# Keys of the second group before the last norm, a split stage of its own, and output weights cast on another engine

## The chip, the cores and the metric

One NeuronCore of one Trainium2 chip runs the whole program. The metric is device time in microseconds of that core, as the median of several executions. Engine names are those of the profile: PE is TensorE's matmul, PEld its weight load, DVE VectorE, ACT ScalarE, POOL GpSimd, and SP the engine that issues most DMAs.

## What is computed

One step of a small encoder: 1024 prompt frames and 32 sample frames, stored together as 1056 columns, model width 1024, two layers. Layer 0 is an mLSTM mixer with a SwiGLU feed-forward; layer 1 is windowed attention with a shared key and value projection, 16 query heads over 2 key heads, a bias per distance and a sink per head, and again a SwiGLU feed-forward. Each sub-layer ends with a LayerNorm.

```python
q = (x @ w_q).reshape(B, nc, CHUNK, N_KV_HEADS, GROUP, HEAD_DIM)
s = einsum('bcqhgd,bckhd->bchgqk', q, k) * HEAD_DIM ** -0.5 + bias
mx = maximum(max(s), sink); p = exp(s - mx)
p = p / (sum(p) + exp(sink - mx))
o = einsum('bchgqk,bckhd->bcqhgd', p, v)
x = layer_norm(alpha * x + o.reshape(B, T, D_ATT) @ w_out, ln_g, ln_b)
```

All of it is float32. The kernel gets that precision from a faster matmul format: every operand is written as a rounded part (hi) and the rest (lo), and each product is three matmuls, hi by hi, hi by lo, lo by hi (lines 416 to 418).

## The kernel before

**Groups and tiles.** The 1056 columns are cut into three groups (0 to 383, 384 to 767, 768 to 1055) for projections, and into four quarters of 264 columns for the norms and the output projection. A projection of one weight tile over one group is 8 steps over the inner dimension, each of three matmuls: 24 matmuls.

**Weave.** All work is issued by one Python program, and the order in which it is issued is the order of each engine's queue. `gemm` (line 408) calls `wv.tick(us)` behind each step of three matmuls, with a nominal time for these. A tick lets side tasks (generators) run whose pauses have run out, and also the weight feed. `wv.drain` runs a task to its end at once. So the pauses of a task fix where, among the matmuls, its instructions stand.

**Weights.** `Weights._next` (line 219) loads a raw tile by SP, casts half of it to the rounded part (hi) and subtracts that to get lo. The cast is on ACT (line 245), or on POOL (line 243) for the halves named in `on_gpsimd`; the subtraction is on POOL, or on DVE for those named in `on_vector` (line 247). Five pairs of buffers hold the results.

**The end of layer 0.** `ffn` leaves four norm tasks, one for each quarter. While the last of them run, the layer-1 projections begin: `keys_values(0)` makes keys and values of group 0, four `q_group(j, 0)` make queries. `tasks[2]` and `tasks[3]`, the norms of quarters 2 and 3, are then drained, the PSUM pool of five banks is closed, and three pools are opened in its place: three banks for projections ("d"), two for scores ("psS", cleared in six single columns by DVE, line 1764), two for transposes ("T") and one for attention outputs ("O").

**The start of attention.** `k_spread` copies each key group to other partitions by six DMAs from SP. It is drained for group 0, then two tasks start: `v_turn(0, 3.0)`, which transposes the values of group 0 into T tiles, of which there are two, and has ACT and DVE split them (lines 1784, 1712 and 1713), and `attention`, which first pauses 4.0. Then `keys_values(1)` and `keys_values(2)` make the keys and values of groups 1 and 2, eight steps each.

**The attention pipeline** (line 1800) goes over 72 items, a head pair's half (j) and a block of 128 rows (b). Its stages: `scores` (PE matmuls into psS, DVE adds the bias and takes the minimum, line 1835), `soft` (ACT exponentials, line 1850), `scale` (DVE reciprocal, and a multiplication that is POOL's for blocks 1 to 7, line 1863), `turn` (PE transposes into a T tile, line 1888, and right behind them the ACT cast to hi, line 1892, and the DVE subtraction to lo, line 1893), `values` (PE matmuls of hi and lo, line 1917, for every second item) and `place` (ACT copy and DVE add). Between rounds it visits the stages in the order given by the last argument: place, turn, scale, soft, scores, values. A pause of 0.46 follows scores and turn.

**The output.** `mixed_parts` splits the attention result into hi and lo (lines 446 and 447, low part on DVE and POOL in turn), `out_tile` multiplies it by the output weights `U_OUT_B[0]` (first two quarters) and `U_OUT_B[1]` (last two). The first three (`EARLY`) tiles of quarter 0 are made between the query projections, the other five while the last attention items run.

Of the kernel before, what the change touches and what calls it, by code (L numbers as in the profile page):

```python
# [16 lines left out]
P = 128  # L17
# [3 lines left out]
DEC = 32  # L21
# [10 lines left out]
EARLY = 3  # L32
# [258 lines left out]
def kernel(ctx: ExitStack, tc: tile.TileContext, A, O):  # L291
    nc = tc.nc
    ctx.enter_context(tc.manual_schedule())
    wv = Weave()
# [11 lines left out]
    def new(p, tag, shape, dt=F32, bufs=1):  # L306
        uid[0] += 1
        return p.tile(list(shape), dt, name=f"{tag}_{uid[0]}", tag=tag, bufs=bufs)
# [45 lines left out]
    U_KV, U_QB, U_OUT_B = [], [[], []], [[], []]  # L354
# [11 lines left out]
    on_vector.update((u, f) for u in U_OUT_B[1][2:] for f in range(2))  # L366
    on_vector.update((u, f) for u in U_Q[:1] for f in range(2))
    on_gpsimd = {(u, 1) for u in U_KV[1] + U_QB[0][4:]}
    on_gpsimd.update((u, f) for u in U_QB[1] + U_OUT_B[0] for f in range(2))
    W = Weights(nc, base, units, pairs, on_vector, on_gpsimd)  # L370
    W.early = {up[i] for up in U_UP for i in range(FIRST, FT)}
    wv.feed = W.feed
# [875 lines left out]
    def out_tile(u, m, cols):  # L1248

        ps = psbank()[:, :N4]  # L1250
        gemm(ps, wcols(u), [(SX[:, 0, k, cols], SX[:, 1, k, cols]) for k in range(KT)])
        z = ACT[:, m, cols]
        nc.vector.scalar_tensor_tensor(z, z, ALPHA, ps, op0=ALU.mult, op1=ALU.add)

    def mixer_out(us, li, lx, opening=None, before=None, made=0):

        box = [lx]

        def run(g, cols, after):
            if before:  # L1260
                before(g)
            if g == 3:
                lx = box[0]
                lx.sums = ExitStack()
                su = lx.sums.enter_context(pool("sums"))
                bufs = [new(su, f"su{i}", [P, 2, N4])[:] for i in range(2)]
                wv.drain(lx.norms[1])
                lx.comb = wv.launch(sums(lx, li, 0, bufs, 2.4))

            order = [6, 7, *range(6)] if g == 3 and not opening else list(range(KT))  # L1270
            for i, m in enumerate(order):
                if not g and m < made:
                    continue
                u = us[g > 0][m]
                W.get(u)
                if g < 2:
                    W.split_to(us[g][min(m + 2, KT - 1)])
                out_tile(u, m, cols)
                if g == 3 or u not in us[1]:
                    W.done(u)  # L1280
                if g == 3 and (u, 0) in W.home:
                    box[0].left += 1
                if box[0]:
                    after(order, i)
            if not box[0]:
                box[0] = opening()
                for i in range(KT):
                    after(order, i)

        return norm_tail(li, run, box), box[0]  # L1290
# [326 lines left out]
    def parts_made(g):  # L1617
        wv.drain(parts, lambda: nparts[0] > g)

    tasks, lx = mixer_out(U_OUT_A, 0, lx, None, lambda g: g < 3 and parts_made(g))  # L1620
    tasks = ffn(0, 1, tasks, lx, False)
# [22 lines left out]
    def k_part(src, c0, n):  # L1644

        dst = slice(c0, c0 + n)
        nc.scalar.copy(KH[0][:, dst], src)
        nc.vector.tensor_sub(KL[0][:, dst], src, KH[0][:, dst].bitcast(F32))
# [60 lines left out]
    def v_parts(c, src, L):  # L1709

        src = src.rearrange("p (g d) -> p g d", g=2)
        nc.scalar.copy(VR[:L, c, :, 0, :], src)
        nc.vector.tensor_sub(VR[:L, c, :, 1, :], src, VR[:L, c, :, 0, :].bitcast(F32))
# [12 lines left out]
    def load_sample_bias(jp):  # L1726

        sb = SB[jp] = new(pb, "sb", [2 * DEC, 2, P + DEC + 1])
        nc.sync.dma_start(sb[:, :, 1:], A["sbias"][:, 2 * jp : 2 * jp + 2, :])
        for h in range(2):  # L1730
            r = slice(DEC * h, DEC * h + DEC)
            nc.gpsimd.tensor_copy(sb[r, :, 0], nsink[r, 4 * jp + h : 4 * jp + 4 : 2])
# [1 line left out]
    load_bias(0)  # L1734
    load_bias(1)
    load_sample_bias(0)
    def keys_values(g):
        if g == 2:
            k_part(ck[:], SEQ, P)
        for f, w in ((k_group, U_KV[g > 0][0]), (v_group, U_KV[g > 0][1])):  # L1740
            f(g)
            if g != 1:
                W.done(w)

    W.pause = 1.3
    for t in tasks[:2]:
# [3 lines left out]
        q_group(j, 0)  # L1750
        W.done(U_QB[0][j])
    W.pause = FEED_W
    for t in tasks[2:]:
        wv.drain(t)
    lx.close()
    lx.zx.close()
    psx[0].close()
# [13 lines left out]
    def pad_values(i, c, g2):  # L1771

        r = slice(64 * i, 64 * i + 64)
        nc.gpsimd.tensor_copy(VZ[i][r, c - 1 + i], VR[r, c, g2].rearrange("p a d -> p (a d)").bitcast(F32))

    def v_turn(group, pause):
        yield pause
        if not group:
            for i in range(2):
                nc.gpsimd.memset(VZ[i][64 * (1 - i) : 64 * (2 - i)].bitcast(F32), 0.0)  # L1780
        for c, c0, L, g, off in CH:
            if g == group:
                pt = new(psb, "T", [P, 512], bufs=2)
                nc.tensor.transpose(pt[:L, :P], vT[g][:, off : off + L], ident[:])
                v_parts(c, pt[:L, :P], L)
                for i in range(2):
                    if 1 - i <= c < 8 - i:
                        pad_values(i, c, 0)
                ast["v"] = c + 1
                yield 0.8  # L1790
# [6 lines left out]
    def last_item(j, g):  # L1797
        return 6 * JG.index((j // 2, g)) + 6

    def attention(gap):  # L1800
        S, pairs_ = {}, {}
# [67 lines left out]
        def blocks(b):  # L1869

            if b == 0:
                return [(1, 130, 64), (2, 258, P)]
            if b == 8:
                return [(0, 2, P), (1, 130, DEC)]
            return [(t, 2 + t * P, P) for t in range(3)]

        def turn(j, b):
            s = S.pop((j, b))
            p = s["p"]
            rows = 2 * DEC if b == 8 else P  # L1880
            if j % 2 == 0:
                pairs_[j // 2, b] = {
                    tag: new(pb2, tag, [P, 2, 3, P], F32R, bufs=2) for tag in ("hi", "lo")
                }
            s = pairs_[j // 2, b]
            pt = new(psb, "T", [P, 512], bufs=2).rearrange("p (t r) -> p t r", t=4)
            for t, at, nk in blocks(b):
                nc.tensor.transpose(pt[:nk, t, :rows], p[:rows, at : at + nk], ident[:rows, :rows])  # L1888
            cuts = [(slice(0, 3), P)] if 0 < b < 8 else [(slice(t, t + 1), nk) for t, _, nk in blocks(b)]
            hi, lo = (s[x][:, j % 2] for x in ("hi", "lo"))  # L1890
            for t, nk in cuts:
                nc.scalar.copy(hi[:nk, t, :rows], pt[:nk, t, :rows])
                nc.vector.tensor_sub(lo[:nk, t, :rows], pt[:nk, t, :rows], hi[:nk, t, :rows].bitcast(F32))
# [25 lines left out]
        def place(j, b):  # L1919
# [12 lines left out]
            for h in range(2):  # L1932
# [4 lines left out]
        always = lambda j, b: True  # L1937
# [5 lines left out]
                (soft, always, 0, 0),  # L1943
                (scale, always, 0, 0),
                (turn, always, 2, (gap,) * 8),
                (values, lambda j, b: ast["v"] > b, 1, (0.0, 2 * gap) * 4),
                (place, always, 0, 0),
            ],
            (5, 3, 2, 1, 0, 4),
        )  # L1950


    for t in spread:
        wv.drain(t)
    wv.launch(v_turn(0, 3.0))
    task = wv.launch(attention(GAP_A))
    ast["ready"] = 4
    for g in range(1, 3):
        keys_values(g)
        wv.launch(v_turn(g, 2.5))  # L1960
    for t in spread:
        wv.drain(t)
# [6 lines left out]
    def q_made():  # L1969
        yield 2.5  # L1970
        ast["ready"] += 1

    def before(g):
        if g == 0:
            wv.drain(task, lambda: ast["placed"] >= last_item(7, 0))
        if g < 3:
            parts_made(g)

    for n, (jp, g) in enumerate(JG):
        if n < 2:  # L1980
            continue
        while ast["scored"] < 6 * (n - 1):
            wv.tick(0.25)
        for j in (2 * jp, 2 * jp + 1):
            q_group(j, g)
            wv.launch(q_made())
            if g != 1:
                W.done(U_QB[g > 0][j])
        if n == 3:
            nparts[0] = 0  # L1990
            parts = wv.launch(
                mixed_parts(
                    scr,
                    lambda g: ast["ready"] > QG.index((7, g)),
                    lambda k, g: ast["placed"] >= last_item(k, g),
                    (2.4, 1.5, 1.5, 1.0, 1.0),
                    (nc.vector, nc.gpsimd),
                    [WHOLE[0], *((g, ks) for ks in (range(6), range(6, KT)) for g in (1, 2))],
                )
            )  # L2000
        if g == 2 and jp < EARLY:
            before(0)
            out_tile(U_OUT_B[0][jp], jp, QUARTERS[0][0])
            W.done(U_OUT_B[0][jp])
# [6 lines left out]
    tasks, lx = mixer_out(U_OUT_B, 2, None, finish, before, EARLY)  # L2011
# [133 lines left out]
```

## Time and profile before

| what | value |
|---|---|
| time, median of 3 runs | 2206.42 us (2204.69 to 2207.07) |
| profiled execution, its own time | 2207.18 us |
| its span in the trace | 2205.4 us |
| PE busy | 2168.4 us, 98% of the span |
| DVE, ACT, POOL busy | 1445.6, 990.7, 976.1 us |

A line of a timeline gives the start in microseconds, the duration, the engine, the line of the kernel and the operation, then output tile and input tiles, and in brackets the idle time before it with what ended it. A line of a table of groups gives the busy sum and the mean of one in ns. `d` is a projection's PSUM tile, `sx` the split activations, `wh` and `wl` (and `oh`, `ex`) split weights, `Q` queries, `KH` and `KL` split keys, `T` transposed tiles, `s` scores and probabilities.

### The profile page before, as it was taken

How to read it: one execution, taken by the hardware profiler on the slowest of the kernel's cores; microseconds unless marked ns; L12 is line 12 of the kernel's file. 1: busy time of each engine (PE TensorE's matmuls, PEld its weight loads, DVE VectorE, ACT ScalarE, POOL GpSimd, SP SyncE). 2: the span in 40 equal slices, each digit the busy share in tenths (PEclk: the TensorE clock that was granted, in tenths of full speed). 3: DMA queues.
4: the chain of work that ended last, by engine and by line, in shares of the span. 5: the costliest groups of instructions: out<-in, count | busy, mean ns of one | idle time of the engine just before them, and what ended most of it. 6: DMA issues, size and time to landing. Idle time of an engine off the chain costs nothing.

```text
span 2205.4 us, 43768 instructions
## 1 busy us (share of the span) xinstructions
PE 2168.4 (98%) x16982; PEld 2141.5 (97%) x16982; DVE 1445.6 (66%) x2818; ACT 990.7 (45%) x2229; POOL 976.1 (44%) x986
## 2 busy tenths in 40 slices
PE   9999999999999999999998999899999999999997
PEld 9999999999999999999998999899999999999997
DVE  4465576787656665566667777788666566467657
ACT  4443455465444444322236676656444444332125
POOL 2554310004655565544526665600666555554441
PEclk9999999999999999999999999999999999999999
DMA  5222212212443443697515321411344434397712
GB/s 170 77 63 57 58 40 87 89 39 77 158 146 138 146 156 137 229 334 232 180 64 151 94 71 51 137 59 39 120 154 156 146 133 151 137 346 252 246 57 80
DMA packets 166192, 289.97 MB, mean 131 GB/s; under 512 B 16416, under 2 KB 121944, under 8 KB 165984
## 3 DMA queue, kind: packets, MB, share of 16 engines
q1 hardware_dynamic: 161632, 282.84, 38.4%
q10 hardware_dynamic: 4352, 4.33, 0.6%
q8 instruction: 134, 2.20, 0.4%
q14 instruction: 74, 0.61, 0.1%
HBM read 202.35 MB, written 82.94 MB: 129 GB/s over the span
## 4 chain that ended last, share of the span: by engine, by line
PE 88%; DVE 6%; ACT 3%; issue 1%; DMA 1%; POOL 1%; SPq 0%; ACTq 0%; DVEq 0%; POOLq 0%
PE d L416 10%; PE d L418 10%; PE d L417 10%; PE A L416 10%; PE A L418 10%; PE A L417 10%; PE B L416 7%; PE B L417 7%; PE B L418 7%; PE O L1917 1%; PE psS L1829 1%; PE T L1888 1%; ACT act L519 1%; DMA hs_x<-z 1%; PE T L969 1%
## 5 line engine op out<-in xcount | busy, mean ns | idle before, releaser
L247 POOL TENSOR_TENSOR wl_s<-wr,wh_s 128x512 fp32r<-128x512 f32 x224 | 304.3, 1368 | 237.4 <-ACT wh_s L245 168.9
L416 PE MATMUL d<-sx,wh 128*128 128x264 f32 (+2 forms) x1040 | 333.5, 321 | 2.9 <-DVE Q L1699 2.2
L247 POOL TENSOR_TENSOR wl_a<-wr,wh_a 128x512 fp32r<-128x512 f32 x112 | 153.2, 1371 | 402.2 <-ACT wh_a L245 396.9
L418 PE MATMUL d<-sx,wl 128*128 128x264 f32 (+2 forms) x1040 | 317.4, 305 | 1.0 <-POOL wl L247 1.0
L417 PE MATMUL d<-sx,wh 128*128 128x264 f32 (+2 forms) x1040 | 316.9, 305 | 0.4 <-DVE sx L447 0.4
L416 PE MATMUL A<-sx,wh_s 128*128 128x264 f32 x896 | 254.5, 284 | 0.0
L417 PE MATMUL A<-sx,wh_s 128*128 128x264 f32 x896 | 254.1, 284 | 0.0
L418 PE MATMUL A<-sx,wl_s 128*128 128x264 f32 x896 | 254.0, 283 | 0.0
L245 ACT CAST wh_s<-wr 128x512 fp32r<-128x512 f32 x224 | 135.9, 619 | 192.4 <-DVE wr L197 102.8
L416 PEld LDWEIGHTS d<-sx,wh 128*128 128x128 f32 x1040 | 197.0, 189 | 6.6 <-ACT act L519 2.5
L417 PEld LDWEIGHTS d<-sx,wh 128*128 128x128 f32 x1040 | 197.3, 190 | 1.5 <-DVE sx L447 0.7
L418 PEld LDWEIGHTS d<-sx,wl 128*128 128x128 f32 x1040 | 196.4, 189 | 1.8 <-POOL wl L247 1.5
L416 PE MATMUL d<-sx,ex 128*128 128x264 f32 x624 | 180.7, 290 | 0.1
L418 PE MATMUL d<-sx,ex 128*128 128x264 f32 x624 | 177.0, 284 | 0.7 <-DVE ex L247 0.7
L417 PE MATMUL d<-sx,ex 128*128 128x264 f32 x624 | 177.2, 284 | 0.0
L418 PEld LDWEIGHTS A<-sx,wl_s 128*128 128x128 f32 x896 | 168.8, 188 | 0.0
L417 PEld LDWEIGHTS A<-sx,wh_s 128*128 128x128 f32 x896 | 168.4, 188 | 0.0
L416 PEld LDWEIGHTS A<-sx,wh_s 128*128 128x128 f32 x896 | 168.4, 188 | 0.0
L1346 POOL TENSOR_TENSOR z<-z 128x528 fp32r<-128x528 f32 x76 | 103.5, 1361 | 126.0 <-ACT z L1345 112.9
L247 POOL TENSOR_TENSOR wl<-wr,wh 128x512 fp32r<-128x512 f32 (+2 forms) x84 | 108.9, 1302 | 85.6 <-ACT wh L245 82.8
L416 PE MATMUL A<-ex,wh_s 128*128 128x264 f32 x448 | 127.5, 285 | 0.0
L417 PE MATMUL A<-ex,wh_s 128*128 128x264 f32 x448 | 127.1, 284 | 0.0
(377 smaller groups left out, 7213.4 us busy)
## 6 DMA issues: line engine op xcount, KB each, us to landing
wr<-in_gu SPq DMA_DIRECT2D x92, 512.0 KB, 4.7
hs_x<-z SPq DMA_DIRECT2D x72, 528.0 KB, 3.0
hs_t<-z SPq DMA_DIRECT2D x64, 528.0 KB, 2.8
sx<-hs_x SPq DMA_DIRECT2D x112, 264.0 KB, 5.9
sx<-hs_t SPq DMA_DIRECT2D x64, 264.0 KB, 6.2
ex<-hs_t SPq DMA_DIRECT2D x64, 264.0 KB, 6.6
wr<-in_dn SPq DMA_DIRECT2D x32, 512.0 KB, 3.9
ex<-hs_x SPq DMA_DIRECT2D x32, 264.0 KB, 5.4
```

What stands on the lines that cost most here:

```text
L245: self.nc.scalar.copy(hi, r)
L247: eng.tensor_sub(lo, r, hi.bitcast(F32))
L416: nc.tensor.matmul(out, ah, bh, start=start and k == 0, stop=False, **kw)
L417: nc.tensor.matmul(out, ah, bl, start=False, stop=False, **kw)
L418: nc.tensor.matmul(out, al, bh, start=False, stop=stop and k == last, **kw)
L519: nc.scalar.activation(z, z, AF.Identity, scale=gk, bias=bk)
L969: nc.tensor.matmul(pc[:, : 2 * (DV + 1)], keys, vt[j][:, c], start=True, stop=True)
L1346: eng.tensor_sub(lo.bitcast(F32R), buf(s), hi)
L1829: nc.tensor.matmul(ps[:rows, at : at + nk], lhs, k[:, k0 : k0 + nk], start=i == 0, stop=i == 1)
L1888: nc.tensor.transpose(pt[:nk, t, :rows], p[:rows, at : at + nk], ident[:rows, :rows])
L1917: nc.tensor.matmul(out, v[:nk], x, start=i == 0, stop=i == len(todo) - 1)
```

## The change

Four things are edited. The keys of group 1 are made after `tasks[2]` has been drained and before `tasks[3]` is, still in the old pool of five banks; only the values of group 1 remain where keys and values stood, and the first pause of `v_turn(0, ...)` goes from 3.0 to 1.0. The cast to hi and the subtraction to lo leave `turn` and become a stage `split`, visited after `soft` and before `scores`. The hi cast of the last five tiles of `U_OUT_B[0]` (ten halves) is no longer in `on_gpsimd`, so it is ACT's. The pause between splits of group 0 in `mixed_parts` goes from 2.4 to 3.0.

```diff
-    on_gpsimd.update((u, f) for u in U_QB[1] + U_OUT_B[0] for f in range(2))
+    on_gpsimd.update((u, f) for u in U_QB[1] + U_OUT_B[0][:EARLY] for f in range(2))
...
-    def keys_values(g):
+    def keys_values(g, todo=(0, 1)):
         if g == 2:
             k_part(ck[:], SEQ, P)
-        for f, w in ((k_group, U_KV[g > 0][0]), (v_group, U_KV[g > 0][1])):
-            f(g)
+        for i in todo:
+            (k_group, v_group)[i](g)
             if g != 1:
-                W.done(w)
+                W.done(U_KV[g > 0][i])
...
-    for t in tasks[2:]:
-        wv.drain(t)
+    wv.drain(tasks[2])
+    keys_values(1, (0,))
+    wv.drain(tasks[3])
     lx.close()
...
                 nc.tensor.transpose(pt[:nk, t, :rows], p[:rows, at : at + nk], ident[:rows, :rows])
+            s["pt"] = pt
+
+        def split(j, b):
+            s = pairs_[j // 2, b]
+            pt = s.pop("pt")
+            rows = 2 * DEC if b == 8 else P
             cuts = [(slice(0, 3), P)] if 0 < b < 8 else [(slice(t, t + 1), nk) for t, _, nk in blocks(b)]
...
                 (turn, always, 2, (gap,) * 8),
+                (split, always, 0, 0),
                 (values, lambda j, b: ast["v"] > b, 1, (0.0, 2 * gap) * 4),
                 (place, always, 0, 0),
             ],
-            (5, 3, 2, 1, 0, 4),
+            (6, 3, 2, 1, 4, 0, 5),
...
-    wv.launch(v_turn(0, 3.0))
+    wv.launch(v_turn(0, 1.0))
     task = wv.launch(attention(GAP_A))
     ast["ready"] = 4
     for g in range(1, 3):
-        keys_values(g)
+        keys_values(g, range(2 - g, 2))
         wv.launch(v_turn(g, 2.5))
...
-                    (2.4, 1.5, 1.5, 1.0, 1.0),
+                    (3.0, 1.5, 1.5, 1.0, 1.0),
```

## Rows read from the trace of the kernel before

**Rows 1.** The page, part 1: busy time, share of the span, instructions by engine.

```profile
PE 2168.4 (98%) x16982; PEld 2141.5 (97%) x16982; DVE 1445.6 (66%) x2818; ACT 990.7 (45%) x2229; POOL 976.1 (44%) x986
```

**Rows 2.** Waits of PE, 1100 to 1600 us: total, times, longest.

```profile
PE T L1888 <- POOL s L1863: 4.0, 2, 2.5
```

**Rows 3.** Stretches at the start of attention: length; busy by engine; PEclk, DMA.

```profile
1190.00:1200.00 10.00, 7.76 (x36) 7.47 (x35) 7.99 (x11) 7.28 (x16) 3.87 (x3) 0.83 0.44 127
1200.00:1210.00 10.00, 5.86 (x28) 5.41 (x27) 6.55 (x28) 6.44 (x19) 4.77 (x10) 0.77 0.45 136
1210.00:1220.00 10.00, 10.00 (x67) 9.57 (x66) 6.60 (x39) 6.37 (x29) 3.69 (x6) 0.89 0.20 50
```

**Rows 4.** Timeline of PE, 1188 to 1208 us.

```profile
1188.52 0.33 PE L416 MATMUL d<-sx,wh 128*128 128x384 f32 x1
...
1192.55 0.34 PE L418 MATMUL d<-sx,wl 128*128 128x384 f32 x1
1195.13 0.66 PE L416 MATMUL d<-sx,wh 128*128 128x384 f32 x1 [2.24 <-DVE Q L1699]
...
1206.00 0.39 PE L1829 MATMUL psS<-KH,Q 128*128 128x64 f32 x1 [4.14 <-issue]
...
1207.95 0.41 PE L1784 MATMUL T<-ident,act 128*128 128x128 f32 x1
```

**Rows 5.** Timeline of DVE, 1204 to 1207 us.

```profile
1204.38 1.12 DVE L1699 SCALAR_TENSOR_TENSOR Q<-d,Q 64x384 fp32r<-64x384 f32 x2
1205.58 0.62 DVE L1764 MEMSET psS<- 128x1 f32 x6
1206.22 0.49 DVE L1713 TENSOR_TENSOR VR<-T,VR 128x128 fp32r<-128x128 f32 x2
1206.63 0.55 DVE L1648 TENSOR_TENSOR KL<-d,KH 128x384 fp32r<-128x384 f32 x1
```

**Rows 6.** Timeline of ACT, the cast of group 1's keys.

```profile
1204.48 0.50 ACT L1647 CAST KH<-d 128x384 fp32r<-128x384 f32 x1
```

**Rows 7.** Timeline of POOL, the last low part of quarter 2.

```profile
1191.70 1.57 POOL L531 TENSOR_TENSOR sx<-act,sx 128x528 fp32r<-128x528 f32 x1 [1.72 <-ACT sx L525]
```

**Rows 8.** Timeline of SP's queue, the second bias table in attention.

```profile
1211.60 0.59 SPq L1720 DMA_DIRECT2D bt<-in_bias  x1
```

**Rows 9.** Timeline of PE, 1397 and 1409 us.

```profile
1397.32 0.55 PE L1888 MATMUL T<-ident,s 128*128 128x128 f32 x3 [1.50 <-POOL s L1863]
...
1409.74 0.55 PE L1888 MATMUL T<-ident,s 128*128 128x128 f32 x3 [2.55 <-POOL s L1863]
```

**Rows 10.** Stretches at the end of attention, columns as in rows 3.

```profile
1385.00:1395.00 10.00, 9.36 (x75) 8.84 (x74) 8.46 (x31) 8.80 (x31) 9.18 (x10) 1.00 0.17 51
1395.00:1405.00 10.00, 8.51 (x74) 8.29 (x73) 6.69 (x26) 6.09 (x21) 9.76 (x12) 1.00 0.46 137
1405.00:1414.00 9.00, 6.45 (x42) 6.24 (x41) 5.13 (x14) 3.88 (x11) 8.69 (x10) 0.81 0.37 117
```

**Rows 11.** Groups of POOL, 1378 to 1409 us: busy sum, mean ns; idle before.

```profile
L243 POOL CAST wh<-wr 128x512 fp32r<-128x512 f32 x7 | 4.9, 695 | 0.0
...
L243 POOL CAST oh<-wr 128x512 fp32r<-128x512 f32 x2 | 1.2, 606 | 0.0
```

**Rows 12.** Waits of PEld, 1212 to 1395 us: total, times, longest.

```profile
PEld psS L1829 <- DVE st L1835: 2.9, 4, 1.3
PEld O L1917 <- ACT hi L1892: 1.9, 3, 1.0
PEld O L1917 <- DVE lo L1893: 1.7, 5, 0.3
```

**Rows 13.** The page, part 5: an ACT cast of half a weight tile.

```profile
L245 ACT CAST wh_s<-wr 128x512 fp32r<-128x512 f32 x224 | 135.9, 619 | 192.4 <-DVE wr L197 102.8
```

**Rows 14.** Groups of ACT, 1380 to 1400 us, columns as in rows 11.

```profile
L1850 ACT ACTIVATE s<-s,st 128x193 f32<-128x193 f32 x14 | 6.3, 451 | 2.0 <-DVE st L1835 2.0
L446 ACT CAST sx<-act 128x384 fp32r<-128x384 f32 (+1 forms) x7 | 3.5, 495 | 0.0
```

## The prediction, made before the run

> **What bounds the kernel now.** I read the page first: PE is busy for 98% of the span [rows 1], so a change that leaves the matmuls alone, as this one does, can only win back PE's idle time and the stretches in which PE's clock is low. The second view is therefore PE's own idle time around the code that is changed. At the start of attention PE stands twice, 2.24 us ahead of the keys of group 1 and 4.14 us ahead of the first scores [rows 4]. At its end it stands twice for a transpose that waits for POOL's scaling [rows 2], 1.50 and 2.55 us [rows 9]. The third view is the stretches. The granted clock falls to a mean of 0.83, 0.77 and 0.89 around the first pair [rows 3] and to 0.81 behind the last wait [rows 10]; in the two stretches between it is 1.00 [rows 10]. As the clock has only the levels 2.4 GHz and 1.2 GHz, a mean of 0.77 over 10 us is 4.6 us at the low one, and the four stretches hold 3.4, 4.6, 2.2 and 3.4 us of it.
>
> What ends those waits is in the other queues. The first scores wait for DVE's clearing of their banks at 1205.58, which stands in DVE's queue behind the last norm and the last queries' eviction at 1204.38 [rows 5]: DVE, not PE, is late there. At the end POOL is busy for 9.18, 9.76 and 8.69 us of stretches of 10, 10 and 9 [rows 10], with no idle time ahead of its weight casts [rows 11]: there POOL sets when a transpose can start.
>
> **Part one, the keys of group 1.** It removes the wait of 2.24 us: this projection now takes a bank of the old pool, and its last operand, the low part of quarter 2, is done at 1193.3 [rows 7], before its seventh step. Twenty-four matmuls take 4.2 us (starts at 1188.52 and 1192.55 are 23 apart, 0.175 us each [rows 4]), so the keys run from 1192.7 to 1196.9. Then come the values of group 1. The pauses say what is mixed in: `v_turn` now starts after 1.0, its transposes stand behind steps 3, 4 and 6 of the values, and attention (4.0 against 8 steps of 0.489) starts only behind the first step of group 2's keys. The third transpose needs the first T tile back, which DVE frees only at line 1713. In DVE's queue the subtraction of these keys (0.55 us, about 0.5 between starts [rows 5]; its ACT half is at 1204.48 [rows 6], in time) now stands ahead of the clearing, so line 1713 goes from 1206.22 to about 1206.7 and PE gets its third transpose at 1207.0. By then PE has made 14 steps of 0.525 us and two transposes and stands since 1200.3. **The two waits become one of 6.7 us.**
>
> Before: 2.24 + 4.14 us idle, and 3.4 + 4.6 + 2.2 us at the low clock, which cost half of that, 5.1 us: 11.5 us in all, some 0.3 us of it counted twice where PE idled at the low clock, so 11.2. After: 6.7 us, and one low stretch. No row shows PE after so long an idle time. The low stretches behind 2.24 and 4.14 us held about 3.4 and 6.2 us of work; if they grow with the idle time (1.5 times it), 10 us follow and cost 5.0; if they don't, 3.4 us cost 1.7. I take 6.2, the one behind the nearest wait, 3.1 us. That makes 9.8 us, **a gain of 1.4 us**, between a loss of 0.5 and a gain of 2.8.
>
> The Trainium skill (TensorE: Matmul & The Clock Gate, section "What's actually happening") has the array come back to the full rate after one sustained busy stretch, however long it idled before. By that the low stretch would not grow, and the gain would lie at the upper bound. The trace has two different lengths behind two different idle times, which the rule leaves to where the idle time falls; I stay with the row.
>
> The step's other instructions: six DMAs of `k_spread` are now issued before attention's first bias table on SP's queue. They wait for the split keys, so that table is issued near 1211, as the second one is now [rows 8]. Its reader is POOL, which fills in the sinks, for item 7's scores near 1217; the cover is about 3 us of other items' work, and if it is gone POOL's scaling is held by as much. I cost it at nothing. Attention starts some four nominal us later against the matmuls, but its later items are held by the queries anyway, so it is level again when group 0's last queries are made.
>
> **Part three, the casts.** (It carries the sum, so it comes before the split.) Ten casts leave POOL. Nine lie between 1378 and 1409 and take 6.1 us, 0.68 each [rows 11]. Four of them stand between 1387 and 1396, ahead of the first late scaling, with POOL busy throughout: the scaling comes 2.7 us earlier, more than the 1.50 us that PE waits. The other four ahead of the second wait give 2.7 us more, against 2.55. Both waits go: 4.05 us. So does the low clock behind the second, 3.4 us, which cost 1.7. Together **5.7 us**. On ACT a cast costs 0.62 us [rows 13]. Between 1385 and 1395 ACT has 1.2 us to spare [rows 10] and gets four casts, 2.5 us, so 1.3 us don't fit; from 1395 on it has room. POOL's subtraction now waits for ACT's cast, and queued behind it on POOL are the scaling and the low parts of `mixed_parts`, for which transposes and output tiles wait. Bounds: nothing, where ACT's lateness falls into its own waits, to 6.2 us, where all ten show on PE. I take the part that doesn't fit, 1.2 us. **A gain of 4.5 us.**
>
> **Part two, the split.** It removes and adds no instruction. ACT's cast to hi no longer stands between an exponential and the one before, waiting for PE's transpose; in return hi and lo come later by a pair of exponentials, about 0.9 us (two of 451 ns, overlapped by their accumulator reads [rows 14]), and `values` waits for them. PE now loses 1.9 us to hi and 1.7 us to lo in eight waits, and 2.9 us to scores that wait for DVE [rows 12]. At best all of that goes, a gain of 6.5; at worst the eight waits grow by 0.9 each, a loss of 7.2. The trace speaks for neither end: between a transpose and its `values` stands mostly one score step and one or two matmul steps, about what hi and lo take. I take nothing.
>
> **Part four, the pause of 3.0.** By the pauses, four of group 0's eight splits instead of three are still open when they are drained ahead of the first output tile. One more ACT cast, 0.5 us [rows 14], is what PE can see of it: **a loss of 0.4 us**, between 0 and 1.
>
> **The sum.** 1.4 + 4.5 - 0.4 = 5.5 us. The profiled execution took 2207.18 us around a span of 2205.4; less 5.5 that is 2201.7. It lies 0.76 us above the median of the three runs, so I forecast **2200.9 us** for the median. Its own range, from the bounds of the start (-0.5 to 2.8) and with up to 2 us of the casts showing (3.7 to 5.7): 2198 to 2203.6.
>
> **The rivals.**
> *The waits move to ACT.* With ten casts more, ACT's queue holds the hi casts, exponentials and weight casts of the last items, and POOL waits for ACT as PE waits for POOL. For it: ACT at 8.80 of 10 us just there. Against it: 3.9 of 10 us free in the next stretch [rows 10]. If half of the casts show on PE, 3.1 us, the gain is 5.7 - 3.1 + 1.4 - 0.4 = 3.6; if the start gives nothing either, 2.2: about 2203.5. Chance 0.28, most of it within 0.2%, which is 4.4 us and about what a measurement of this kernel can tell from no change.
> *The split frees the middle too.* Exponentials that no longer wait for transposes bring the reciprocals, scalings and transposes forward, and half or more of the 6.5 us in the middle go: 2194.5 to 2197.5. For it: 2.0 us of ACT's idle time ahead of exponentials ends with DVE [rows 14], which ACT feeds in turn. Chance 0.15.
> *The split starves the values (slower).* Of 36 `values` steps, those whose hi and lo come 0.9 us later than their place in PE's queue stop PE. Eight stop it already. Against the gain of 5.5 it decides from 7 such steps; at 11 of them the change is 4.4 us slower, at 14 it gives 2208. The place is the first score step behind each second transpose. For it: ACT is the fullest just where the casts are added. Against it: exponentials that come early make their own transposes early. Chance 0.10 for slower by more than 0.2%, 0.06 for a smaller loss.
> *The early keys buy nothing,* because the third transpose or the clearing is later than I have it, DVE's queue being the same: then 1.4 us are missing and the rest holds, 2202.3. It is in the forecast's range.
>
> **How the numbers follow.** The forecast has 0.41, the deeper gain 0.15, the moved waits 0.28, the starved values 0.16. Faster by over 0.2% (below 2202.0): 0.32 of the forecast, all of the deeper gain, and 0.10 of the moved waits, 0.57. Slower by over 0.2% (above 2210.8): 0.10. Within: 0.33. For 8 in 10 the range goes down to 2194.5 and up to 2207.0, which leaves out the starved values and the farthest of the deeper gain.
>
> **What would show it.** Start: PE's waits of 2.24 and 4.14 us gone and one of 6 to 7 us ahead of the third transpose of line 1784, released by DVE's line 1713, near 1207; a single low stretch in the granted clock. End: no wait of line 1888 for line 1863 above 0.5 us between 1390 and 1410, POOL with idle time in every stretch there, clock 1.00; ACT above 9 of 10 us between 1385 and 1395, and POOL's line 247 waiting for ACT's line 245. Middle: PE's waits ahead of line 1917 within 1 us of the 3.6 us now. The prediction is wrong if the wait at the start stays two, if line 1888 still waits for POOL at the end, or if line 1917 waits for more than 6 us in all.

## The result, and the profile after

| | median, us | lowest to highest |
|---|---|---|
| before (5 runs) | 2206.58 | 2204.69 to 2207.07 |
| after (5 runs) | 2216.64 | 2215.81 to 2218.62 |

The ratio is 1.0047 with a 95% interval of 1.0033 to 1.0062: the change makes the kernel 10.1 us **slower**. The profiled execution took 2216.64 us around a span of 2214.9 us, 9.5 us more than the span before.

The page, part 1, of the kernel after: busy time, share of the span, instructions [rows 1].

```profile
PE 2173.3 (98%) x16982; PEld 2143.3 (97%) x16982; DVE 1444.3 (65%) x2818; ACT 997.1 (45%) x2239; POOL 969.4 (44%) x976
```

The work is the same; ten casts have gone from POOL to ACT. Waits of PE, 1190 to 1440 us, in the kernel after: total, times, longest [rows 2, 4].

```profile
PE T L1785 <- DVE VR L1713: 6.5, 1, 6.5
PE O L1924 <- DVE lo L1900: 4.3, 12, 1.4
PE O L1924 <- ACT hi L1899: 3.8, 5, 1.9
PE T L1785 <- DVE lo L1900: 1.9, 2, 1.0
```

The two waits for POOL's scaling are gone, and at the start one wait of 6.5 us has taken the place of two. In their stead attention's output tiles (`O`, line 1924 now) wait for hi and lo, 8.1 us in 17 waits. The same in the waits of PEld, 1212 to 1395 us [rows 12]:

```profile
PEld O L1924 <- DVE lo L1900: 5.1, 13, 0.9
PEld O L1924 <- ACT hi L1899: 3.4, 7, 1.1
PEld T L1785 <- DVE lo L1900: 2.4, 2, 1.3
```

The first two are 8.5 us in 20 waits where it was 3.6 us in eight. In the third the transposes of the values wait for a T tile, of which there are two: lo, which frees one, comes later. The stretches of the kernel after, first those of [rows 3], then of [rows 10]; PEclk is the third number from the end:

```profile
1190.00:1200.00 10.00, 10.00 (x58) 9.60 (x56) 7.71 (x11) 7.28 (x16) 3.92 (x3) 1.00 0.44 140
1200.00:1210.00 10.00, 3.50 (x14) 3.50 (x14) 5.97 (x18) 4.87 (x12) 4.41 (x8) 0.69 0.41 113
1210.00:1220.00 10.00, 8.84 (x68) 8.31 (x67) 6.17 (x39) 6.93 (x32) 4.79 (x10) 0.97 0.09 24
1385.00:1395.00 10.00, 9.69 (x73) 8.83 (x72) 6.44 (x31) 7.52 (x26) 5.14 (x6) 1.00 0.18 54
1395.00:1405.00 10.00, 7.84 (x51) 7.43 (x51) 6.62 (x23) 8.85 (x28) 8.55 (x9) 0.84 0.33 106
1405.00:1414.00 9.00, 9.00 (x77) 8.90 (x76) 6.36 (x23) 6.54 (x20) 7.67 (x8) 0.99 0.49 149
```

POOL now has time to spare at the end, and yet PE stands and loses its clock there (0.84). Two more stretches of the kernel after lose it; before, both were at 1.00, and the one low stretch at the end was that of [rows 10]:

```profile
1290.00:1300.00 10.00, 7.82 (x47) 7.20 (x46) 7.13 (x24) 6.34 (x18) 8.48 (x10) 0.83 0.26 79
1420.00:1430.00 10.00, 8.71 (x53) 7.97 (x53) 6.15 (x17) 3.70 (x11) 2.72 (x4) 0.83 0.35 111
```

**Where the time goes.** The 36 `values` steps are the same in every kernel, so the start of one of them says how late PE is by then. The starts of four of them after, in the timeline of PEld:

```profile
1253.03 0.19 PEld L1924 LDWEIGHTS O<-hi,VR 128*128 128x128 f32 x1 [0.33 <-ACT hi L1899]
...
1301.68 0.19 PEld L1924 LDWEIGHTS O<-hi,VR 128*128 128x128 f32 x1
...
1394.06 0.19 PEld L1924 LDWEIGHTS O<-hi,VR 128*128 128x128 f32 x1
...
1429.16 0.19 PEld L1924 LDWEIGHTS O<-hi,VR 128*128 128x128 f32 x1
```

Before, the same steps started at 1252.77, 1295.16, 1386.44 and 1419.57. So PE is 0.3 us late at the first, 6.5 at the second, 7.6 at the third and 9.6 at the last: next to nothing at the start, 6.3 us between 1253 and 1295, 2.0 us at the end, where the casts had been expected to gain 4.5 us. The same table for the kernels of the next section (us behind before at that step, from one profiled execution each):

| kernel | 1252.77 | 1295.16 | 1386.44 | 1419.57 | median against before |
|---|---|---|---|---|---|
| after | +0.3 | +6.5 | +7.6 | +9.6 | +10.1 |
| early keys alone | +2.4 | +3.4 | +3.4 | +3.4 | +3.3 |
| split alone | +0.5 | +5.7 | +6.7 | +4.3 | +5.2 |
| casts alone | -0.6 | -0.7 | -0.7 | -5.8 | -5.0 |
| pause alone | -0.3 | +0.1 | 0.0 | 0.0 | -0.1 |
| all but the keys | +0.4 | +4.1 | +5.2 | +7.3 | +7.4 |
| all but the split's stage | +0.6 | +3.3 | +3.3 | -1.8 | -0.2 |
| split ahead of exponentials | -0.1 | +3.0 | +2.7 | +1.9 | +2.3 |
| that, with the casts | +0.6 | +2.1 | +1.8 | -3.3 | -2.1 |

### The profile page after: what moved, and what is told of

Its sections match the earlier page's. It is cut to its first block, busy times and chain, and to the rows that moved or that the text cites. A ratio compares the mean times of both kernels' runs of the same rounds, so it can differ in the third digit from the quotient of the medians.

```text
span 2214.9 us, 43764 instructions
## 1 busy us (share of the span) xinstructions
PE 2173.3 (98%) x16982; PEld 2143.3 (97%) x16982; DVE 1444.3 (65%) x2818; ACT 997.1 (45%) x2239; POOL 969.4 (44%) x976
## 4 chain that ended last, share of the span: by engine, by line
PE 83%; DVE 7%; ACT 5%; DMA 3%; issue 1%; SPq 0%; POOL 0%; ACTq 0%; DVEq 0%
PE d L416 10%; PE d L418 10%; PE d L417 10%; PE A L416 9%; PE A L417 9%; PE A L418 9%; PE B L416 7%; PE B L417 7%; PE B L418 7%; DMA sx<-hs_t 1%; PE O L1924 1%; ACT s L1851 1%; ACT act L519 1%; DVE Q L1699 1%; DMA hs_x<-z 1%
```

## The experiments

Each time is a median over five rounds, its ratio against before measured beside it on the same chip.

**The parts, each alone.** First the early keys: `keys_values(1, (0,))` between the two drains, and the pause of `v_turn(0, ...)` at 1.0.

> The kernel before with the keys of group 1 moved and the first pause of v_turn at 1.0, nothing else. Theory (the split is what costs): 1 to 3 us faster than before, with one wait of about 6.8 us for the third value transpose and none of the four waits (1.1, 0.5, 1.3, 0.7 us) that the changed kernel shows between 1216 and 1233 us. Rival (the early keys thin out the matmuls beside the first items): those four waits are there, and it is 0 to 2 us slower.

Measured: 2210.05 us, ratio 1.0015 (1.0007 to 1.0024). A loss is there, as the rival asked, but by the median it is larger than the rival's 0 to 2 us, and of the rival's four waits only one has its like (1.4 us near 1220). The start went as forecast (one wait, 6.7 us, for line 1713); the loss stands behind it. SP's queue and POOL in this kernel, timelines:

```profile
1209.40 0.58 SPq L1720 DMA_DIRECT2D bt<-in_bias  x1
...
1226.02 0.59 SPq L1720 DMA_DIRECT2D bt<-in_bias  x1
```

```profile
1221.24 0.83 POOL L1864 TENSOR_TENSOR s<-s,st 128x384 f32<-128x384 f32 x1
1229.37 0.41 POOL L1724 COPY bt<-nsink 64x4 f32<-64x4 f32 x2 [7.30 <-DMA bt<-in_bias]
...
1230.52 0.82 POOL L1864 TENSOR_TENSOR s<-s,st 128x384 f32<-128x384 f32 x1
```

The *second* bias table, issued at 1211.60 before [rows 8], is now issued at 1226.02, behind the copies of group 2's keys on SP. POOL stands 7.3 us for it, with a scaling queued behind, and PE stands for that scaling (2.2 us of PEld's idle time, 1.9 of PE's own); behind it the clock is 0.83 from 1230 to 1240. In the kernel after POOL has the same wait, 6.6 us to 1227.75, but there PE, held by lo before, comes to that transpose only at 1229.95 and doesn't wait.

The split alone:

```diff
+            s["pt"] = pt
+        def split(j, b): ...
+                (split, always, 0, 0),
-            (5, 3, 2, 1, 0, 4),
+            (6, 3, 2, 1, 4, 0, 5),
```

> The kernel before with the split as a stage behind the exponentials, nothing else. Theory (the split is what costs): 6 to 10 us slower, with over 6 us of PE waiting at the values' matmuls for hi and lo (2.3 us in the kernel before by PE's own count of waits). Rival (the longer pause of mixed_parts or the casts cost): within 2 us of before.

Measured: 2212.02 us, ratio 1.0025 (1.0015 to 1.0036): 5.2 us slower, by the median a little under the theory's 6 to 10 (the interval, 3.3 to 7.9, reaches it), with 6.3 us of PE's waits for hi and lo between 1190 and 1440 us. ACT's timelines around the largest step, first before, then the split alone:

```profile
1287.66 0.58 ACT L1931 COPY t<-O 64x512 f32<-64x512 f32 x1
1288.27 0.48 ACT L1892 CAST hi<-T 128x384 fp32r<-128x384 f32 x1
1288.65 0.52 ACT L446 CAST sx<-act 128x384 fp32r<-128x384 f32 x1
1289.54 0.93 ACT L446 CAST sx<-act 128x384 fp32r<-128x384 f32 x2 [0.37 <-DVE act L1935]
1290.37 0.46 ACT L1850 ACTIVATE s<-s,st 128x193 f32<-128x193 f32 x1
```

```profile
1290.93 0.58 ACT L1937 COPY t<-O 64x512 f32<-64x512 f32 x1
1291.41 0.51 ACT L446 CAST sx<-act 128x384 fp32r<-128x384 f32 x1
1292.87 0.93 ACT L446 CAST sx<-act 128x384 fp32r<-128x384 f32 x2 [0.94 <-DVE act L1941]
1293.70 0.45 ACT L1850 ACTIVATE s<-s,st 128x193 f32<-128x193 f32 x1
...
1294.15 0.44 ACT L1850 ACTIVATE s<-s,st 128x193 f32<-128x193 f32 x1
...
1294.71 0.48 ACT L1898 CAST hi<-T 128x384 fp32r<-128x384 f32 x1
```

Before, hi came straight behind the copy of O. Now three casts of line 446, 0.94 us in which these wait for DVE, and a pair of exponentials stand between: hi starts 3.8 us after the copy instead of 0.6, and PE waits 2.3 us for it. At the end the split alone wins something back (6.7 us late at 1386.44, 4.3 at 1419.57): one of the two waits for POOL's scaling is gone there.

The casts alone (`U_OUT_B[0][:EARLY]` in place of `U_OUT_B[0]`), and the pause of 3.0 alone:

> The kernel before with the ten casts on ScalarE, nothing else. Theory (the casts are a gain that the split hides): 3 to 6 us faster, no transpose waiting for POOL's scaling at the end. Rival (the waits move to ScalarE): within 2 us of before, with PE waiting for hi between 1390 and 1420 us.

> The kernel before with the pause of 3.0 between the splits of group 0, nothing else. Theory (the split is what costs): 0 to 1 us slower. Rival (the burst of four splits ahead of the first output tile costs the wait of 1.3 us and the low clock behind it that the changed kernel shows near 1292 us): 2 to 5 us slower.

Measured: the casts 2201.78 us, ratio 0.9979 (0.9970 to 0.9988), a gain of 5.0 us; the pause 2206.68 us, ratio 1.0000 (0.9992 to 1.0009). Stretches at the end with the casts alone [rows 10]:

```profile
1385.00:1395.00 10.00, 8.81 (x71) 8.29 (x70) 6.63 (x25) 9.89 (x33) 9.06 (x9) 1.00 0.25 75
...
1405.00:1414.00 9.00, 8.86 (x69) 8.05 (x67) 7.53 (x20) 6.05 (x17) 6.14 (x6) 1.00 0.51 171
```

The clock is whole, and ACT is full: 9.89 of 10 us. Its price on PE is one wait for hi of 1.0 us. With the pause alone PE does stand for the burst that the rival names, 1.5 us at 1289.86 for a low part that `mixed_parts` makes (DVE, line 447), but it is level with before again at 1295.

The four parts alone add to 3.3 + 5.2 - 5.0 - 0.1 = 3.4 us. The whole change costs 10.1, so 6.7 us come from parts acting on each other; some of it is that the split and the casts both win at the waits for POOL's scaling at the end, which can be won only once. The next two runs ask which parts meet.

**All but the keys.**

> The whole change but without the early keys (split, casts and the pause of 3.0 stay). Theory (the late split and the casts both stand on ACT's queue ahead of the hi casts of the last items, so the 5.0 us that the casts alone gained are lost again): 4 to 8 us slower than before; between 1386 and 1420 PE loses at least 1 us against before where the casts alone won 5.1, in waits of output tiles for hi and lo. Rival (the effects add: +5.2 for the split, -5.0 for the casts, 0 for the pause): within 1.5 us of before.

Measured: 2214.13 us, ratio 1.0034 (1.0022 to 1.0047), 7.4 us slower where the parts add to 0.1. The theory holds: the split and the casts (with the pause, which does nothing alone) spoil each other, without the keys. ACT's timeline in this kernel, from 1393.8 us:

```profile
1393.84 1.18 ACT L1696 ACTIVATE Q<-d 64x256 fp32r<-64x256 f32 x4
1395.04 0.62 ACT L245 CAST oh<-wr 128x512 fp32r<-128x512 f32 x1
1395.57 1.13 ACT L245 CAST wh<-wr 128x512 fp32r<-128x512 f32 x2
1396.61 0.26 ACT L1937 COPY t<-O 64x128 f32<-64x128 f32 x1
1396.77 0.46 ACT L1850 ACTIVATE s<-s,st 128x193 f32<-128x193 f32 x1
...
1397.78 0.48 ACT L1898 CAST hi<-T 128x384 fp32r<-128x384 f32 x1
```

PE in the same kernel, the transposes of which this hi is made, and the output step that needs it:

```profile
1393.61 0.49 PE L1888 MATMUL T<-ident,s 128*128 128x128 f32 x3
...
1398.31 0.38 PE L1923 MATMUL O<-hi,VR 128*128 128x256 f32 x1 [1.99 <-ACT hi L1898]
```

ACT never stands between the two: in the 3.7 us from the end of the transposes to hi it does a query's eviction, three weight casts that used to be POOL's, a copy and a pair of exponentials. The casts take 1.75 us of it, the exponentials 1.0.

The other long wait at the end, 1.4 us at 1418.87, is one for lo, and it is not ACT's: hi was cast at 1415.91. On DVE lo stands behind the additions of `place` and a scaling; the order of the stages (split behind `scale`) has put the scaling ahead of it:

```profile
1417.18 1.18 DVE L1867 TENSOR_SCALAR s<-s,st 64x160 f32<-64x160 f32 x1
1418.28 0.54 DVE L1899 TENSOR_TENSOR lo<-T,hi 128x384 fp32r<-128x384 f32 x1
```

What the end costs in all shows in one stretch from the step at 1386.44 to that at 1419.57, first with the casts alone, then in all but the keys:

```profile
1385.73:1413.76 28.03, 26.70 (x215) 25.42 (x214) 21.64 (x73) 24.59 (x71) 24.47 (x24) 1.00 0.47 144
1391.67:1426.88 35.21, 30.64 (x215) 28.65 (x214) 23.62 (x78) 24.88 (x71) 23.66 (x23) 0.90 0.36 115
```

PE does the same 215 matmuls in 28.0 and in 35.2 us (33.1 before, 30.7 with the split alone). Of the 7.2 us between the two, 3.2 are idle time (4.6 against 1.3 us) and 3.9 longer busy time, at a mean granted clock of 0.90 instead of 1.00. The low clock behind the waits costs about as much as the waits.

**All but the split's stage.**

> The whole change but without the split's stage (early keys, casts and the pause stay). Theory (the split is what spoils the casts; the keys' loss is at the start, far from the casts): the sum of the keys' +3.3 and the casts' -5.0, so 1 to 3 us faster than before. Rival (the casts lose their gain to the early keys or the pause as well): over 1 us slower than before.

Measured: 2206.56 us, ratio 1.0000 (0.9991 to 1.0009): neither. The parts add to -1.8 us; the interval (2 us either way) reaches that far, so the size of what is left over is not settled. The table says where it is not: at the end the casts' gain is whole (from +3.3 to -1.8). Between 1253 and 1295 this kernel loses 2.7 us, where the early keys alone lose 1.0; PE stands 1.5 us there for the burst of the pause, and behind it the clock is 0.83. In its waits of PEld, 1250 to 1440 us, those of `values` for hi and lo are close to before (3.6 us in eight), 4.4 us in nine:

```profile
PEld O L1918 <- ACT hi L1893: 2.4, 3, 1.2
PEld O L1918 <- DVE lo L1894: 2.0, 6, 0.4
```

against the same view of all but the keys, 12.8 us in 22:

```profile
PEld O L1923 <- DVE lo L1899: 7.2, 15, 1.6
PEld O L1923 <- ACT hi L1898: 5.6, 7, 2.2
```

**What of the split costs.** The stage stays behind the pause of the transposes, but is visited ahead of the exponentials, and so stands ahead of them in ACT's queue.

```diff
-            (6, 3, 2, 1, 4, 0, 5),
+            (6, 3, 4, 2, 1, 0, 5),
```

> The split as a stage of its own behind the transposes' pause, but taken up ahead of the exponentials and the scaling instead of behind them (order 6, 3, 4, 2, 1, 0, 5). Theory (what costs is that a pair of exponentials and a weight's rounding stand ahead of hi on ACT): within 1.5 us of before, and no wait of 2 us for hi near 1293. Rival (what costs is the pause that now lies between a transpose and its split): 4 to 6 us slower, like the split alone.

Measured: 2209.06 us, ratio 1.0009 (1.0001 to 1.0018), 2.3 us slower: between the two by the median, and the interval (0.2 to 4.0) touches both. The order gives back 2.9 of the 5.2 us. The wait near 1290 is still there, 1.5 us, since the casts of line 446 now get in during the pause; behind it the clock is 0.83 in this execution, where it was 1.00 with the split alone. So it seems that both rivals hold a part: the exponentials, and whatever is issued in the pause between a transpose and its split.

With the casts added to this order:

> The casts on ScalarE together with the split's stage taken up ahead of the exponentials (order 6, 3, 4, 2, 1, 0, 5), nothing else. Theory (the casts lose their gain because a pair of exponentials stands ahead of hi, on top of the casts): the two effects add, +2.3 and -5.0, so 1.5 to 4 us faster than before. Rival (the pause between a transpose and its split lets weight casts in ahead of hi, whatever the order): 0 to 4 us slower than before, with output tiles waiting for hi by 1.5 us or more between 1386 and 1420.

Measured: 2204.75 us, ratio 0.9991 (0.9982 to 1.0000), 2.1 us faster: the effects add (2.3 - 5.0 = -2.7), as the theory has it. Taking the exponentials from ahead of hi gives the casts their gain back: in ACT's queue the same query's eviction, three weight casts and copy still stand ahead of the hi at 1393.32, but no exponentials, and PE waits 1.0 us for it instead of 2.0. This kernel also lacks the pause of 3.0 that all but the keys has; split and casts without that pause, in the order of the change, were not run, but by the table the pause alone does nothing behind 1295. Its waits of PEld, 1250 to 1440 us, are 6.3 us in ten:

```profile
PEld O L1923 <- ACT hi L1898: 3.8, 3, 1.7
PEld O L1923 <- DVE lo L1899: 2.5, 7, 0.5
```

**What of the keys costs.** POOL's copy of the sinks into a bias table goes ahead of the table's DMA instead of behind it; the columns are others, so the order is free.

```diff
+            nc.gpsimd.tensor_copy(bt[r, :, 0 : WK + 2 : WK + 1], ...)
         nc.sync.dma_start(bt[:, :, 1 : WK + 1], ...)
-            nc.gpsimd.tensor_copy(bt[r, :, 0 : WK + 2 : WK + 1], ...)
```

> The early keys alone, and POOL fills the sinks into a bias table before the table's DMA is issued instead of after it, so that POOL never waits for the DMA. Theory (in the early keys' kernel the second table's DMA is issued 14 us later, behind the DMAs of group 2's keys, and POOL stands 7.3 us for it, so a transpose waits 2.2 us for its scaling): 1.5 to 3 us faster than the early keys alone, that is 0 to 1.8 us slower than before; the wait of 2.2 us near 1231 is gone. Rival (the loss is the long wait at 1200 to 1207 and its low clock): the same as the early keys alone, 3 us slower than before.

> The early keys, the casts on ScalarE and the sinks filled in before the bias table's DMA is issued; no split stage, the pause as before. Theory (the fill takes away what the early keys cost POOL, and keys and casts add): +1.0 and -5.0, so 3 to 5 us faster than before, not faster than the casts alone. Rival (the casts lose some of their gain to the shifted start of attention, as in the kernel without the split's stage): 0 to 2.5 us faster than before.

Measured: with the early keys 2207.73 us, ratio 1.0003 (0.9994 to 1.0012), 2.3 us better than without the fill (the two intervals overlap), and the wait of 2.2 us is gone although the table still comes late (1227.61). With keys and casts 2203.17 us, ratio 0.9984 (0.9976 to 0.9993): -3.6 where 1.0 - 5.0 = -4.0 was expected. Keys and casts add; what the early keys cost was mostly the table. But even so they gain nothing: with the fill too PE loses 1.0 us between 1253 and 1295, as with the early keys alone (+2.4 to +3.4), and why was not followed.

**Can the early keys gain at all?** Two versions of this last kernel give PE more to do ahead of the long wait: `v_turn(0, 3.0)` again, or `v_turn(0, 5.0)` and attention's first pause 6.0 instead of 4.0.

> As the early keys with casts and fill, but the value transposes of group 0 keep their pause of 3.0 instead of 1.0. Theory (the 6.5 to 7 us wait ends with VectorE at a fixed time near 1206, so whatever PE is given ahead of it shortens it): the wait at the start is 1 to 2.5 us shorter, and the kernel 1 to 2 us faster than the same kernel with the pause of 1.0. Rival (what PE is given ahead is missing behind, while the scalings of the first items are made): no difference within 1 us.

> The same with the value transposes of group 0 after a pause of 5.0 and attention's first scores after 6.0 instead of 4.0, so that several steps of group 2's keys stand ahead of both. Theory (as above): the wait at the start falls to 2 to 4 us and the kernel is 2 to 4 us faster than with the pause of 1.0, and faster than the casts alone. Rival (the first items come later and PE waits for them instead, or attention ends later): not faster than the casts alone.

Measured: 2201.09 us, ratio 0.9975 (0.9965 to 0.9985), and 2201.51 us, ratio 0.9975 (0.9965 to 0.9984). The wait at the start fell from 6.5 to 4.5 and to 2.6 us (idle time of PEld), as the theory says. The first gained 2.1 us by it. The second gained 1.7, less than the 2 to 4 expected: it is 3.8 us ahead of before at 1253 but level with it at 1295, with new waits of 1.6 and 1.3 us near 1282. These two are the fastest kernels measured here, and faster than both before and after; by their intervals they can't be told from the casts alone (0.9970 to 0.9988).

## Why the prediction was wrong

**Part one, the start.** The mechanism was right: one wait, released by line 1713, at 1206.50, of 6.5 us by PE's waits (6.7 predicted), and one low stretch. Its size was a little under the forecast. By the granted clock of the kernel after (0.88, 0.50 and 0.94 in the three stretches of 5 us from 1200) 6.8 us were at the low level; taken as one stretch it ends at 1210.6, 4.1 us of work behind the wait, where 6.2 had been put down. By the prediction's own way of counting that makes 6.5 + 2.05, 8.6 us against 11.2 before, so at this place the gain was 2.6 and not 1.4.

The rule of the Trainium skill that the prediction cited (TensorE: Matmul & The Clock Gate, "What's actually happening") said that the low stretch would not grow with the idle time, and the trace agrees: 4.1 us of work behind a wait of 6.5 us, against 6.2 behind 4.14. Both low stretches last 6.8 us in all (4.6 and 2.2 in [rows 3]); after the change more of it lies in the wait.

What failed is the sentence on SP's queue, "I cost it at nothing". It followed the first bias table, which was indeed issued near 1209. It didn't follow the second, which moved by 14 us behind the next group's copies; POOL waited 7.3 us for it in the keys' own kernel. "If it is gone POOL's scaling is held by as much" was the right price for the wrong table. And attention was not simply "level again": with the fill too PE stands 1.4 us ahead of transposes of early items, at 1221.87, where it did not stand before. PEld's row names no releaser; PE's own names DVE's lo, which frees a T tile, and ACT casts and copies group 2's keys just ahead of its hi. That attention's later start has put them there is argued and not shown. Gain of 1.4 expected, loss of 3.3 (1.5 to 5.3) measured alone.

**Part three, the casts.** Right in mechanism and size, alone: 4.5 expected, 5.0 measured, both waits for POOL and the low stretch gone, ACT at 9.89 of 10 us. Wrong in company.

**Part two, the split.** "I take nothing" is the term that broke the forecast: 5.2 us alone. The step behind it, that one score step and one or two matmul steps are "about what hi and lo take", was read from an ACT queue in which hi stood right behind the transposes' own stage. It priced the delay as one pair of exponentials, 0.9 us. In truth hi also falls behind all that is issued in the pause: casts of line 446 with their own wait for DVE, and, with the casts, an eviction and weight casts; and lo, on DVE, behind a scaling. In the rows shown it comes 3.2 us later than before.

**The sum itself** is the second fault. The terms were priced one by one against the queue of before and added, although two of them put work on ACT ahead of the same hi. The parts alone add to +3.4 us; the 6.7 us more are this meeting, as large, within the intervals, as the 7.3 us that it makes without the keys. Nor did the sum count a low clock behind new waits, which is about half of the price at the end (3.9 of 7.2 us). The rival "the split starves the values" described it, with its place on ACT and the casts named, but it had a chance of 0.16, and its argument against it ("exponentials that come early make their own transposes early") has only this for it, that the split alone wins 2.4 us at the end. One of its prices doesn't follow from its own sum: at 14 steps of 0.9 us against 5.5 the change is 7.1 us slower, some 2213.5 us, and 2208 belongs to eight. It decided from 7 steps, at 0.9 us each; the waits of PEld between 1212 and 1395 show 12 more than before, 4.9 us more in all, 0.4 each: more steps at a smaller price, and then the end of attention as well.

**Part four, the pause.** 0.4 expected, 0 measured (-1.8 to 2.0): within its bounds, but not by its mechanism. What PE sees is not one ACT cast of 0.5 us. All four kernels with the pause of 3.0 have a wait for a low part of `mixed_parts` near 1290, 1.1 to 1.5 us, and no other kernel has it; with the pause alone PE is level with before again just behind it (+0.1 us at 1295), and what pays for it was not followed. That the size came out is luck.

**What would show it** named the right sign: the output tiles' waits above 6 us. They are 8.5 us by the measure of [rows 12], which gave the 3.6. The clock at the end, 0.84 where 1.00 had been asked for, was another.

## What to carry to other kernels

Where two edits put work on the same in-order queue ahead of the same small producer, price them together: list what stands between the producer's input and the producer after both edits. Two edits that shorten the same wait can win it only once. Moving a stage behind a pause costs all that other tasks issue into that pause, not only what it was moved behind. When a step with DMAs moves, follow every later DMA of that queue to its reader, not only the next one.

## What was not expected of the hardware

The clock did not follow the idle time alone. In the version with the latest transposes PE stood 2.6 us ahead of 1207.25, and the granted clock stayed whole; before, a wait of the same size (2.5 us of PEld's idle time, to 1195.10) was followed by 0.83 in [rows 3]. The stretches of that version:

```profile
1200.00:1210.00 10.00, 7.68 (x57) 7.45 (x55) 7.26 (x27) 7.00 (x21) 4.19 (x8) 1.00 0.50 149
1210.00:1220.00 10.00, 8.62 (x62) 7.62 (x62) 7.98 (x41) 7.62 (x35) 7.81 (x15) 1.00 0.46 125
```

Likewise 1290 to 1300 us with all but the keys, where PE is busy for 7.83 us as after it is for 7.82:

```profile
1290.00:1300.00 10.00, 7.83 (x58) 7.16 (x57) 6.92 (x26) 6.83 (x22) 8.90 (x11) 1.00 0.26 79
```

Here the clock is 1.00, there 0.83, which is 3.4 us at the low level and costs at most half of that, 1.7 us.

Nor is it the program alone that decides. With the casts alone PE does at the start what it does before, and stands 2.3 us for the same eviction of queries. Before, the stretch had 0.83 [rows 3]; here:

```profile
1190.00:1200.00 10.00, 7.61 (x43) 6.93 (x42) 7.76 (x11) 7.32 (x16) 3.87 (x3) 1.00 0.41 133
```

With the pause alone and the split alone it is 0.83 again, with all but the keys 1.00. So a single profiled execution can have up to 1.7 us in such a stretch that another need not have, and a forecast should give it a chance, not a certainty. What decides it was not tried.
